# A two-layer Hyena and attention block whose instructions are put in order by the scheduler's timeline model

## The chip, the cores and the metric

The kernel runs on one core of a Trainium2 chip. The core has five engines that each work through a queue of their own in order: PE (TensorE, matrix products), DVE (VectorE), ACT (ScalarE), POOL (GpSimd) and SP (SyncE, which here only issues DMAs). They meet through semaphores. The metric is the device time of one execution in microseconds (us); a kernel's time is the median of its runs.

## What is computed

The reference is a block of two layers over 512 latent tokens and 256 context tokens of width 1024, in float32. Layer 0 is a Hyena mixer (a long convolution by FFT), layer 1 is grouped-query attention. Cut to its core:

```python
def hyena_mixer(h, w_in, conv_w, conv_b, ..., d_skip, w_out):
    proj = h @ w_in                                       # 1024 -> 4 x 2048
    x0, x1, v = split(short_conv(proj[..., :3 * E_HY], conv_w, conv_b), 3)
    z = proj[..., 3 * E_HY:]
    u = x1 * v
    k = hyena_filter(L, ...)                              # per channel, over |k| summed
    y = irfft(rfft(u, 2 * L) * rfft(k, 2 * L))[:L]
    y = (y + u * d_skip) * x0
    return (y * silu(z)) @ w_out

def gqa_mixer(h_lat, h_ctx, w_in, q_g, k_g, w_out):
    q, k, v, z = ...                                      # 16 heads of 128, 4 key heads
    q, k = rope(rms_norm(q)), rope(rms_norm(k))           # context keys carry no position
    o = softmax(q @ k_all.T / sqrt(128)) @ v_all          # 512 queries, 768 keys
    return (o * silu(z)) @ w_out

def reference(x, c, ctx, c_ctx, ...):
    for i in range(2):
        sh, sc, gt = split(silu(c) @ ada_w[i] + ada_b[i], 3)
        h = rms_norm(x, norm_g[i]) * (1 + sc) + sh        # the same for ctx with c_ctx
        x = x + gt * (hyena_mixer if i == 0 else gqa_mixer)(h, ...)
    return x
```

## The kernel before

A float32 matrix is carried as two fp32r parts, a high and a low one, and a product is three matmuls: high by high, high by low, low by high. In the input projection of the Hyena layer (`in_step`, L465 to L470) one step of the contraction is therefore six matmuls, three of 512 columns for the latents (tile `pl...`) and three of 256 for the context (`pc...`), and eight steps make one projection of 128 channels. ACT makes the high part of a weight (`whi`, L121), POOL the low part (`wlo`, L122).

**The Hyena layer** runs over eight groups g of 256 channels, each of two chunks i = 2g, 2g+1 of 128. A group is one period of some 99 us, from about 100 to 850 us of the profile. In a period PE computes for each chunk the projections `plx1`, `plv`, `plz`, `plx0`. The short convolution behind each (`conv`) is one ACT instruction (L512) and four DVE instructions (L513 and L515, each for latents and context), which read the projection out of its bank of PSUM. u = x1 v is transposed (`ut`, L537 and after) and brought to the frequency domain (`pu`, `fwd`, L550). The filter of the next group is made beside it: `pk` (`lags`, L377 to L382, six per group), a norm (`knorm`, L395, a DVE reduction), folding on POOL (F, L428 to L435) and its transform `ks` (L441, ending in DVE's `kt`, L452). DVE multiplies spectra (`ab...`, `times`, L560, then L584) and folds them (`Y`, L569, L570); `pq` (`y_stage`, L616) is the way back, ACT scales its second half (`qs`, L624), DVE adds and subtracts (L625, L626) and finishes y (L628, L629). The modulation vectors of the second layer are summed on DVE in this stretch too (`adaacc`, L198), from 512-KB pieces that SP fetches (`adas`).

**Two rings of four PSUM banks** feed these: `mmt` (L157) for the projections, `axt` (L160) for everything else, `pk`, `ks`, `ut`, `pu` and `pq` among it. A tile that takes a bank waits until the readers of the tile that had it four tiles earlier are through:

```python
    def axt(name):
        return pa.tile([P, 512], F32, tag="ax", name=name, bufs=4)
```

**The attention layer** (about 1000 us to the end) runs over eight pairs p of heads, 64 blocks n of 128 queries. `score` (L1088) computes `sc` on PE, DVE takes the row maximum (L1099, L1100), ACT the exponential `E` with its sum (L1102), DVE divides (L1103, L1104). `turn` (L1107) transposes E on PE (`et`, L1114), ACT copies it to `pth` (L1118) and DVE takes the low part `ptl` (L1119). `mix` (L1121) multiplies two such blocks with the values (`po`). Projections for later pairs (`pq`, `pz`) and the output product (`px`) stand between. `sc` and `et` share a ring of two PSUM tiles (`s3`, L995), so a score waits for the tile used two before it, and E has two buffers.

**The order.** The program is written as one stream in which the stages of a period are laid by hand between the steps of the projections (a table of slots at the loop over g). That stream is not the order on the engines: the framework's `TileContext` collects all instructions, its scheduler chooses an order for each engine's queue, and only then are buffers' waits turned into semaphores. In the kernel before, the scheduler goes by a plain list of ready times. The engines then follow the order chosen, strictly, each its own queue.

## Time and profile before

| | us |
|---|---|
| runs | 1512.92, 1518.78, 1520.66 |
| median | 1518.78 |
| the profiled execution, its own time | 1517.56 |
| its span, first to last instruction | 1515.7 |
| PE busy | 1455.5 (96%) |
| DVE busy | 1183.7 (78%) |
| ACT busy | 547.5 (36%) |
| POOL busy | 513.9 (34%) |
| mean granted TensorE clock, share of full | 0.983 |

Busy is the time in which an engine had an instruction under way. Matmuls are pipelined: of two back to back of 512 columns the second starts 0.23 us after the first, though each is shown with 0.39 to 0.40 us, so PE's idle time is shorter than the distance between two starts. TensorE's clock has two levels, 2.4 and 1.2 GHz, written as 1.00 and 0.50; a number between them is a mean over a stretch. "Idle before" is the time in which an engine had nothing under way, and the releaser is the instruction that ended it.

### The profile page before, as it was taken

What the parts mean: (1) busy time and instruction counts of PE and PEld (TensorE: products, weight loads), DVE (VectorE), ACT (ScalarE), POOL (GpSimd) and SP (SyncE); (2) the same over time, 40 slices, a digit from 0 to 9 for tenths busy, and PEclk for the clock granted to TensorE, in tenths of its full rate; (3) what the DMA queues carried; (4) which work ended last, traced back from release to release, by engine and by line L of the source; (5) the groups of instructions that cost most, each with busy time, mean ns of one, the idle gap of its engine ahead of it and who ended that gap; (6) DMA issues with size and microseconds to landing.
All of it is one profiled execution on the core that took longest, in us unless ns stands there. A gap on an engine that the chain in (4) does not pass through costs nothing.

```text
span 1515.7 us, 22866 instructions
## 1 busy us (share of the span) xinstructions
PE 1455.5 (96%) x8787; PEld 1263.9 (83%) x8787; DVE 1183.7 (78%) x2004; ACT 547.5 (36%) x1057; POOL 513.9 (34%) x449
## 2 busy tenths in 40 slices
PE   8998999989999999999999999999999999999998
PEld 1787987878878878789888787799998998998987
DVE  5769879889789888987969644575787878878886
ACT  3431322313223223223232334543545544544542
POOL 2462744626537354264464343121110000000005
PEclk9999999999999999999999999999999999999999
DMA  8612223232232232223233667246232212212111
GB/s 298 189 50 83 78 77 91 77 93 86 74 105 69 85 87 70 87 85 90 84 98 108 236 218 260 72 123 214 85 112 70 82 58 70 84 57 70 44 64 74
DMA packets 150783, 157.45 MB, mean 104 GB/s; under 512 B 6953, under 2 KB 122212, under 8 KB 150164
## 3 DMA queue, kind: packets, MB, share of 16 engines
q1 hardware_dynamic: 146324, 134.76, 28.7%
q0 software_dynamic: 4208, 20.72, 4.0%
q8 instruction: 69, 1.13, 0.3%
q10 hardware_dynamic: 144, 0.52, 0.1%
q14 instruction: 38, 0.31, 0.1%
HBM read 138.14 MB, written 17.84 MB: 103 GB/s over the span
## 4 chain that ended last, share of the span: by engine, by line
PE 60%; DVE 23%; issue 5%; POOL 5%; DMA 4%; ACT 2%; SPq 0%; POOLq 0%; ACTq 0%; DVEq 0%
PE po L70 4%; PE po L72 4%; PE po L71 4%; DVE adaacc L198 3%; PE et L1114 3%; DMA adas<-in_ada_w_dram 2%; PE px L70 2%; PE pz L70 2%; PE px L72 2%; PE pz L72 2%; PE px L71 2%; PE pz L71 2%; PE pq L70 2%; PE pq L72 2%; PE pq L71 2%
## 5 line engine op out<-in xcount | busy, mean ns | idle before, releaser
L122 POOL TENSOR_TENSOR wlo<-stg,whi 128x1024 fp32r<-128x1024 f32 x64 | 159.3, 2489 | 260.9 <-ACT whi L121 256.6
L121 ACT CAST whi<-stg 128x1024 fp32r<-128x1024 f32 x99 | 103.8, 1049 | 233.6 <-PE pcz L468 81.1
L873 POOL TENSOR_TENSOR r2q<-s2q,mhalf 128x2 f32<-128x2 f32 x32 | 23.4, 731 | 343.6 <-DVE s2q L871 332.4
L465 PE MATMUL plx<-h_hi,whi 128*128 128x512 f32 x248 | 104.1, 420 | 8.1 <-DVE cvx L515 8.1
L198 DVE SCALAR_TENSOR_TENSOR adaacc<-adas,sil,adaacc 128x512 f32<-128x512 f32 x98 | 102.8, 1053 | 10.9 <-DMA adas<-in_ada_w_dram 10.6
L1102 ACT ACTIVATE E<-sc,st 128x768 f32<-128x768 f32 x64 | 57.7, 902 | 126.9 <-DVE st L1100 114.1
L469 PE MATMUL plx<-h_hi,wlo 128*128 128x512 f32 x248 | 101.3, 409 | 0.0
L466 PE MATMUL plx<-h_lo,whi 128*128 128x512 f32 x248 | 101.3, 408 | 0.0
L467 PE MATMUL pcx<-hc_hi,whi 128*128 128x256 f32 x248 | 72.5, 292 | 4.7 <-DVE cvx L515 4.6
L1099 DVE TENSOR_REDUCE st<-sc 128x1 f32<-128x768 f32 x64 | 61.0, 953 | 17.5 <-PE sc L72 17.2
L468 PE MATMUL pcx<-hc_lo,whi 128*128 128x256 f32 x248 | 71.7, 289 | 0.0
L470 PE MATMUL pcx<-hc_hi,wlo 128*128 128x256 f32 x248 | 71.5, 288 | 0.0
L752 DVE TENSOR_TENSOR yl<-yf,yh 128x768 fp32r<-128x768 f32 x26 | 25.7, 990 | 51.9 <-ACT yh L751 51.8
L1119 DVE TENSOR_TENSOR ptl<-et,pth 128x768 fp32r<-128x768 f32 x64 | 61.1, 954 | 5.3 <-ACT pth L1118 4.0
L465 PEld LDWEIGHTS plx<-h_hi,whi 128*128 128x128 f32 x248 | 49.2, 198 | 18.7 <-issue 8.8
L467 PEld LDWEIGHTS pcx<-hc_hi,whi 128*128 128x128 f32 x248 | 49.2, 198 | 18.5 <-issue 4.9
L1118 ACT CAST pth<-et 128x768 fp32r<-128x768 f32 x64 | 51.1, 798 | 31.1 <-PE et L1114 31.0
L468 PEld LDWEIGHTS pcx<-hc_lo,whi 128*128 128x128 f32 x248 | 49.1, 198 | 11.3
L465 PE MATMUL plv<-h_hi,whi 128*128 128x512 f32 x120 | 49.4, 412 | 5.5 <-DVE cvv L515 5.5
L72 PE MATMUL po<-pth,kvt 128*128 128x256 f32 x192 | 54.1, 282 | 0.0
L71 PE MATMUL po<-ptl,kvt 128*128 128x256 f32 x192 | 54.0, 281 | 0.0
L70 PE MATMUL po<-pth,kvt 128*128 128x256 f32 x192 | 53.9, 281 | 0.0
(909 smaller groups left out, 5181.5 us busy)
## 6 DMA issues: line engine op xcount, KB each, us to landing
stg<-in_hy_w_in_dram SPq DMA_DIRECT2D x64, 512.0 KB
stg<-in_at_w_in_dram SPq DMA_DIRECT2D x40, 512.0 KB
adas<-in_ada_w_dram SPq DMA_DIRECT2D x32, 512.0 KB
yf<-y_scr POOLq DMA_DIRECT2D x32, 384.0 KB, 5.0
ad<-in_ada_w_dram SPq DMA_DIRECT2D x16, 512.0 KB
stg<-in_hy_w_out_dram SPq DMA_DIRECT2D x16, 512.0 KB
stg<-in_at_w_out_dram SPq DMA_DIRECT2D x16, 512.0 KB
dec<-in_k_dec_dram SPq DMA_DIRECT2D x48, 128.0 KB
```

Source lines behind the costliest of these rows:

```text
L70: TE.matmul(ps, lh, rh, start=first, stop=False)
L71: TE.matmul(ps, lh, rl, start=False, stop=False)
L72: TE.matmul(ps, ll, rh, start=False, stop=last)
L121: S.copy(hi, st)
L122: (lo_eng or lo_default[0]).tensor_tensor(lo, st, f(hi), ALU.subtract)
L198: V.scalar_tensor_tensor(accs[n_], sv[:, k, :], sc, accs[n_], ALU.mult, ALU.add)
L465: TE.matmul(pl, hi[:, k, :], h_hi[:, k, :], start=fi, stop=False)
L466: TE.matmul(pl, hi[:, k, :], h_lo[:, k, :], start=False, stop=False)
L467: TE.matmul(pc[:, 0:LC], hi[:, k, :], hc_hi[:, k, :], start=fi, stop=False)
L468: TE.matmul(pc[:, 0:LC], hi[:, k, :], hc_lo[:, k, :], start=False, stop=False)
L469: TE.matmul(pl, lo[:, k, :], h_hi[:, k, :], start=False, stop=la)
L470: TE.matmul(pc[:, 0:LC], lo[:, k, :], hc_hi[:, k, :], start=False, stop=la)
```

## The change

The context in which the program is recorded gets one flag. With it the scheduler orders each block against its timeline model, a model of when each engine would start and end each instruction, in place of the plain list of ready times.

```diff
-    with tile.TileContext(nc) as tc:
+    with tile.TileContext(nc, schedule_with_timeline_sim=True) as tc:
         hybrid_kernel(tc, *args, out)
```

No instruction is added, removed or reshaped: both programs have 8473 on PE, 2006 on DVE, 884 on ACT, 454 on POOL and 384 on SP. What differs is the place of each in its queue, and with it the semaphores. Three places follow. Names of tiles end in a running number; the part ahead of it is the name in the code with its group, chunk or block.

**PE, at the `pk` of group 4** (`plx0_7` is the projection of x0 for chunk 7, `plx1_8` that of x1 for chunk 8). Before:

```order
L469 MATMUL plx0_7_3955<-h_hi_69,wlo32_3951 128x512
L470 MATMUL pcx0_7_3956<-hc_hi_71,wlo32_3951 128x256
L379 MATMUL pk4_0_3998<-w4h4_3984,h3_194 128x512
L380 MATMUL pk4_0_3998<-w4l4_3985,h3_194 128x512
L379 MATMUL pk4_1_4004<-w4h4_3984,h3_194 128x512
L380 MATMUL pk4_1_4004<-w4l4_3985,h3_194 128x512
L465 MATMUL plx0_7_3955<-h_hi_69,whi32_3950 128x512
L466 MATMUL plx0_7_3955<-h_lo_70,whi32_3950 128x512
```

After, at the first and at the second `pk`:

```order
L465 MATMUL plx0_7_3955<-h_hi_69,whi32_3950 128x512
L466 MATMUL plx0_7_3955<-h_lo_70,whi32_3950 128x512
L379 MATMUL pk4_0_3998<-w4h4_3984,h3_194 128x512
L380 MATMUL pk4_0_3998<-w4l4_3985,h3_194 128x512
L467 MATMUL pcx0_7_3956<-hc_hi_71,whi32_3950 128x256
L468 MATMUL pcx0_7_3956<-hc_lo_72,whi32_3950 128x256
L469 MATMUL plx0_7_3955<-h_hi_69,wlo32_3951 128x512
```

```order
L470 MATMUL pcx1_8_4079<-hc_hi_71,wlo33_4074 128x256
L465 MATMUL plx1_8_4078<-h_hi_69,whi33_4073 128x512
L379 MATMUL pk4_1_4004<-w4h4_3984,h3_194 128x512
L380 MATMUL pk4_1_4004<-w4l4_3985,h3_194 128x512
L466 MATMUL plx1_8_4078<-h_lo_70,whi33_4073 128x512
L467 MATMUL pcx1_8_4079<-hc_hi_71,whi33_4073 128x256
L468 MATMUL pcx1_8_4079<-hc_lo_72,whi33_4073 128x256
```

Before, the second `pk` stands right behind the first. After, it stands 29 rows behind it, among the steps of the next projection; the remaining four follow at distances of 7 to 19 rows, where before it was 8.

**DVE, in the y step of chunk 6** (it reads `pq6` and finishes y; `mx4_0` is the norm's reduction of group 4, `cvx1_8` the short convolution that frees the bank of `plx1_8`). Before:

```order
L515 SCALAR_TENSOR_TENSOR cvx0_7_4064<-pcx0_7_3956,vb_81,cvx0_7_4064 128x255
L626 SCALAR_TENSOR_TENSOR y6_4126<-pq6_0_4112,rn_87,qs6_0_4127 128x2x128
L605 TENSOR_TENSOR cvx0_7_4064<-cvx0_7_4064,sz7_3946 128x768
L625 SCALAR_TENSOR_TENSOR y6_4126<-pq6_1_4113,rn_87,qs6_1_4131 128x128
L626 SCALAR_TENSOR_TENSOR y6_4126<-pq6_1_4113,rn_87,qs6_1_4131 128x128
L198 SCALAR_TENSOR_TENSOR adaacc_1_512_0_3697<-adas_1_512_3_4383,sil_82,adaacc_1_512_0_3697 128x512
L628 SCALAR_TENSOR_TENSOR y6_4126<-cvx1_6_3266,vb_81,y6_4126 128x768
L198 SCALAR_TENSOR_TENSOR adaacc_1_512_0_3697<-adas_1_512_3_4383,sil_82,adaacc_1_512_0_3697 128x512
L629 TENSOR_TENSOR y6_4126<-y6_4126,cvx0_6_3840 128x768
L198 SCALAR_TENSOR_TENSOR adaacc_1_512_1_3700<-adas_1_512_3_4383,sil_82,adaacc_1_512_1_3700 128x512
L395 TENSOR_REDUCE mx4_0_4428<-kfl4_3988 128x256
L513 SCALAR_TENSOR_TENSOR cvx1_8_4168<-plx1_8_4078,vb_81,cvx1_8_4168 128x511
```

After:

```order
L395 TENSOR_REDUCE mx4_0_4428<-kfl4_3988 128x256
L513 SCALAR_TENSOR_TENSOR cvx1_8_4168<-plx1_8_4078,vb_81,cvx1_8_4168 128x511
L513 SCALAR_TENSOR_TENSOR cvx1_8_4168<-pcx1_8_4079,vb_81,cvx1_8_4168 128x255
L382 TENSOR_TENSOR kfc4_3989<-pk4_5_4054,dec4_5_4052 128x512
L386 MEMSET kfc4_3989 1x256
L625 SCALAR_TENSOR_TENSOR y6_4126<-pq6_0_4112,rn_87,qs6_0_4127 128x2x128
L626 SCALAR_TENSOR_TENSOR y6_4126<-pq6_0_4112,rn_87,qs6_0_4127 128x2x128
L515 SCALAR_TENSOR_TENSOR cvx1_8_4168<-plx1_8_4078,vb_81,cvx1_8_4168 128x511
L515 SCALAR_TENSOR_TENSOR cvx1_8_4168<-pcx1_8_4079,vb_81,cvx1_8_4168 128x255
```

Before, the whole y step stands ahead of the convolution of `plx1_8`. After, the convolution's first half stands ahead of the y step and its second half behind the first two instructions of it; the `adaacc` rows have gone to an earlier place.

**PE, in the last pair of heads** (`sc63` is the last score, `et61` the transposes of block 61, `px6` the output product of pair 6). Before:

```order
L72 MATMUL px6_2_0_14741<-whx134_14472,ohl6_14076 128x512
L1114 MATMUL et61_14751<-ident_60,E61_14669 128x128 x6
L70 MATMUL px6_2_1_14774<-whi133_14466,ohl6_14076 128x512
L71 MATMUL px6_2_1_14774<-wlo133_14467,ohl6_14076 128x512
L72 MATMUL px6_2_1_14774<-whi133_14466,ohl6_14076 128x512
L70 MATMUL px6_2_1_14774<-whx134_14472,ohl6_14076 128x512
L71 MATMUL px6_2_1_14774<-wlx134_14473,ohl6_14076 128x512
L72 MATMUL px6_2_1_14774<-whx134_14472,ohl6_14076 128x512
L70 MATMUL po30_14784<-pth60_14706,kvt3_13089 128x256
L70 MATMUL px6_3_0_14818<-whi133_14466,ohl6_14076 128x512
L71 MATMUL px6_3_0_14818<-wlo133_14467,ohl6_14076 128x512
L70 MATMUL sc63_14760<-kvt3_13089,qh7_14063 128x512
```

After, from the last matmul of `sc62`:

```order
L71 MATMUL sc62_14727<-kvt3_13089,qh7_14063 128x256
L72 MATMUL sc62_14727<-kvt3_13089,ql7_14064 128x256
L1114 MATMUL et61_14751<-ident_60,E61_14669 128x128 x6
L70 MATMUL sc63_14760<-kvt3_13089,qh7_14063 128x512
L71 MATMUL sc63_14760<-kvt3_13089,qh7_14063 128x512
```

Before, products `px6` and the head of `po30` stand between `et61` and `sc63`, and six more `px6` between `sc62` and `et61`. After, `sc63` follows `sc62` with only `et61` between.

At the head, SP issues all loads of x and three further pieces (two of `dec`, and `kinv`) ahead of most pieces of `ad`, the first layer's modulation weights; before, these stood behind them. At the end, the last output products `px7` are finished close together instead of one after the other.

## Rows read from the trace of the kernel before

**Rows 1.** The page: span, busy time by engine, GB/s in 40 slices.

```profile
span 1515.7 us, 22866 instructions
...
PE 1455.5 (96%) x8787; PEld 1263.9 (83%) x8787; DVE 1183.7 (78%) x2004; ACT 547.5 (36%) x1057; POOL 513.9 (34%) x449
...
GB/s 298 189 50 83 78 77 91 77 93 86 74 105 69 85 87 70 87 85 90 84 98 108 236 218 260 72 123 214 85 112 70 82 58 70 84 57 70 44 64 74
```

**Rows 2.** Windows: stretch, length, busy us by engine, TensorE clock, DMA share, GB/s.

```profile
0.00:100.00 100.00, 89.64 (x386) 53.95 (x387) 67.12 (x122) 39.90 (x78) 46.72 (x60) 0.95 0.62 198
100.00:850.00 750.00, 707.15 (x4263) 621.83 (x4263) 641.99 (x856) 211.49 (x346) 360.98 (x258) 0.97 0.29 87
850.00:1000.00 150.00, 147.14 (x720) 121.38 (x720) 80.70 (x139) 65.06 (x112) 49.07 (x69) 1.00 0.55 186
1000.00:1516.00 516.00, 511.55 (x3424) 466.71 (x3422) 393.88 (x890) 231.03 (x521) 57.11 (x63) 1.00 0.27 86
```

**Rows 3.** Waits of PE: line, what released it; total us, times, longest.

```profile
PE plx L465 <- DVE cvx L515: 8.1, 4, 2.7
PE plv L465 <- DVE cvv L515: 5.5, 5, 3.4
PE pcx L467 <- DVE cvx L515: 4.6, 2, 3.4
PE pk L379 <- DVE ab411a L560: 3.2, 1, 3.2
...
PE pk L379 <- DVE ab211a L560: 1.7, 1, 1.7
```

**Rows 4.** Timeline of PE: start, duration, instruction, [idle before it <- releaser].

```profile
431.00 0.39 PE L465 MATMUL plx<-h_hi,whi 128*128 128x512 f32 x1
432.05 0.40 PE L465 MATMUL plx<-h_hi,whi 128*128 128x512 f32 x1
...
433.34 0.40 PE L380 MATMUL pk<-w4l,h 128*128 128x512 f32 x1
436.60 0.48 PE L379 MATMUL pk<-w4h,h 128*128 128x512 f32 x1 [2.87 <-DVE ab311a L560]
...
468.22 0.28 PE L470 MATMUL pcv<-hc_hi,wlo 128*128 128x256 f32 x1
471.16 0.77 PE L465 MATMUL plx<-h_hi,whi 128*128 128x512 f32 x1 [2.65 <-DVE cvx L515]
```

**Rows 5.** Windows on two stretches at a lower TensorE clock.

```profile
147.00:151.00 4.00, 4.00 (x15) 3.28 (x14) 4.00 (x7) 0.00 (x0) 0.00 (x0) 0.59 0.30 91
822.00:830.00 8.00, 6.55 (x22) 5.67 (x23) 7.96 (x9) 0.87 (x2) 3.92 (x2) 0.57 0.40 131
```

**Rows 6.** Timeline of DVE around the y steps of one period.

```profile
454.12 0.48 DVE L625 SCALAR_TENSOR_TENSOR y<-pq,rn,qs 128x256 f32<-128x256 f32 x1 [4.01 <-ACT qs L624]
...
457.82 3.51 DVE L628 SCALAR_TENSOR_TENSOR y<-cvx,vb,y 128x768 f32<-128x768 f32 x1
...
465.49 3.82 DVE L395 TENSOR_REDUCE mx<-kfl 128x256 f32<-128x2048 f32 x1
469.22 0.74 DVE L513 SCALAR_TENSOR_TENSOR cvx<-plx,vb,cvx 128x511 f32<-128x511 f32 x1
...
477.07 1.02 DVE L628 SCALAR_TENSOR_TENSOR y<-cvx,vb,y 128x768 f32<-128x768 f32 x1
```

**Rows 7.** Timeline of POOL in the same stretch.

```profile
458.12 2.39 POOL L122 TENSOR_TENSOR wlo<-stg,whi 128x1024 fp32r<-128x1024 f32 x1
```

**Rows 8.** Groups of DVE, 100 to 850 us: busy, mean ns, idle before.

```profile
L198 DVE SCALAR_TENSOR_TENSOR adaacc<-adas,sil,adaacc 128x512 f32<-128x512 f32 x96 | 100.8, 1054 | 10.9 <-DMA adas<-in_ada_w_dram 10.6
```

**Rows 9.** Timeline of DVE in attention.

```profile
1441.13 0.68 DVE L1064 TENSOR_TENSOR x<-x,px 128x512 f32<-128x512 f32 x1
...
1456.68 0.96 DVE L1099 TENSOR_REDUCE st<-sc 128x1 f32<-128x768 f32 x1 [0.19 <-PE sc L72]
...
1458.95 0.17 DVE L1103 RECIPROCAL st<-st 128x1 f32<-128x1 f32 x1 [1.12 <-ACT E L1102]
```

## The prediction

> **What bounds the kernel now.** I read the page first: PE is busy for 1455.5 of 1515.7 us [rows 1], so an order can give back at most PE's idle time and its time at the lower clock. The windows tell where these lie [rows 2]. From 100 to 850 us, the Hyena periods, PE is busy 707.15 of 750 us and idle 42.9; in attention it is idle 4.5 of 516, most of it behind the last matmul. So the stretch that can gain is Hyena, and attention can only lose. The list of PE's waits names the idle time [rows 3]: seven waits of `pk` for an `ab` product of DVE, from 3.2 to 1.7 us, sum 19.7; and waits of the projections for the convolution that frees their bank, 8.1 + 5.5 + 4.6 = 18.2. The rest, 5 us, is scattered. The timeline then shows one of each kind [rows 4]: PE stands from 433.34 to 436.60 at the second `pk`, and from 468.22 to 471.16 at a `plx`.
>
> Neither is a lack of DVE time: DVE is busy 642 of 750 us [rows 2], 84.8 in a period of 99.1 (7.57 of these in the stretch). It is the order of its queue. In the second case DVE idles 4.01 us for the `qs` of a y step, then works that step off, with one instruction of 3.51, and a reduction of 3.82, and only at 469.22 begins the convolution that PE needs [rows 6].
>
> The waits cost a second time. After each of the long waits (the shortest is 2.8 us) the granted clock falls to the lower of its two levels, 1.2 GHz, for a stretch. The first such stretch reads 0.59 over 4 us, or 1.6 us of full-speed work lost; the last, a double one, 0.57 over 6.55 us of work, or 2.8 [rows 5]. There are eleven from 100 to 850: 10 x 1.6 + 2.8 = 19 us. Waits of 1.8 us or less had none.
>
> **The change part by part.** Nothing is added or removed, so every term is a wait that goes, comes or grows. I set the sum against the profiled execution's 1517.6 us, 1.2 below the median of the runs. For a wait in the new order I add the durations that the trace gives to the instructions between the two points on both queues, and take what the waiting engine is early by.
>
> *Waits that go.* Before, the second `pk` stood right behind the first. Now 29 rows stand between, nearly five steps of six matmuls at 1.05 us each (431.00 to 432.05) [rows 4]: 5 us of PE work where 3.3 were stood idle. The convolutions now stand ahead of the y step or within it, so `plx` no longer waits behind the 4.0 of idle time, the 3.51 and what lies between [rows 6]. By this addition the Hyena waits left in the new order are five: 1.3 (a `pk`), 1.7 (a `pu`), 1.2 (a `ks`), 2.7 (the `po` at the end) and 1.7 (a `pq`), together 8.6.
>
> *Waits that come in Hyena.* The y step is later, and its two banks of the `axt` ring with it; that is in the 8.6. The sums of `adaacc` stand up to 35 rows earlier in DVE's queue, ahead of the `ab400a` products. They waited 10.6 us in all for their DMA before, over 96 instructions [rows 8]. Earlier in the queue they meet two pieces in series and DVE idles about 4.5 us a period there, an estimate from the issue of a piece to its first use, some 4 us. What reaches PE lies between nothing (DVE has 14 us of slack in a period) and 3.5 us a period, 24.5 in seven; I take 1 a period, 7 us, nearer the low end because the old waits of this kind, though 10.6 us long, name no wait of PE. The folding on POOL feeds `ks` with 0 to 1 us to spare; bounds 0 and 14 us, taken 2. Hyena idle time is then 8.6 + 7 + 2 = 17.6 in place of 42.9: **25 us less**.
>
> *The clock.* Waits long enough for a drop remain at the `po` and perhaps at two others: 4 us in place of 19, **15 less**. Bounds: 5 if a wait near 3 us stays in every period, 19 if none does.
>
> *Attention.* Here the new order is tighter. A score may begin when the exponential of the score before it has left their bank. From the end of `sc` to the end of E the trace shows about 2.4 us: the reduction begins 0.19 after PE at 1456.68, E is over at 1458.95 [rows 9]. Before, the PE work between one score and the next was 3.6 us or more in all but two places (2.3 and 1.6). Now it is 2.05 in seven places and 0.66 in three, where only the transposes stand between (and 1.4 where it was 1.6): 7 x 0.35 + 3 x 1.75 = 7.7. Three transposes (`et`) come 1.1 early and one `po` 1.0, together 4.3. **12 more.** Bounds: 6, if part of these waits gives DVE time that the next one uses, and 20, if the queue of DVE, busy 394 of 516 us [rows 2], runs late at some of the others. None is long enough for the clock.
>
> *Head, border and tail.* At the head some 0.5 MB more go ahead of the last `ad`: at the 298 GB/s of the first slice [rows 1] 1.7 us, bounds -1 and 2. From 850 to 1000 PE is idle 2.9 us [rows 2] and its order changes throughout: 0, bounds -2.9 and 3. At the end the last products finish together, with additions of 0.68 [rows 9] behind each other: 1, bounds 0 and 2. **3 more.**
>
> Sum: 1517.6 - 25 - 15 + 12 + 3 = 1492.6; with the 1.2 to the median, about 1494.
>
> *A rule against it.* DVE's L628 took 3.51 us at 457.82 and 1.02 at 477.07; beside the first, POOL was in a subtraction from 458.12 to 460.51 [rows 6, 7]. The Trainium skill (SBUF — State Buffer, "SBUF: two separate sides") says that a DVE instruction with two SBUF inputs and a GpSimd instruction that reads SBUF share a port pair which one holds for its whole length while the other waits. By that rule, the trace agrees: L628 ended at 461.33, 0.8 after POOL's instruction. An order that puts more of DVE's two-input work beside POOL then makes DVE slower, which the second rival prices.
>
> **The rivals.** *Best case:* only the 8.6 stay in Hyena, all dips go, attention loses 6, the edges nothing: 1517.6 - 34.3 - 19 + 6 = 1470, or 1471. For it: DVE's slack. Against: the waits for POOL and DMA.
>
> *DVE held up by POOL.* A period has six instructions like L628 (L605, L628, L629 of two chunks). If two more of them meet POOL, each adds 2.5 us [rows 6]: DVE at 89.8 a period, and with some 6 us of waits for ACT that the new order doesn't take out, 96 of the 99.1. Hyena then gives 7.57 x 3.1 = 23 in place of 40, and the time is 1517.6 - 23 + 15 = 1510, or 1511. Against: the order of POOL changes little.
>
> *Attention becomes the loss* (slower). Place: the waits of `sc`, `et` and `po`. In the new order 39 of 263 stand under 1 us of slack; before it was 14. If DVE comes to each of the 39 a time x later than this addition says, the kernel loses 39x more. It is slower by over 0.5% from 25 + 7.6 = 39x on, x = 0.84 us; at x = 1.2 the time is 1492.6 + 47 = 1540. For it: DVE's busy share. Against: one `L1099` is 0.96 us [rows 9], and DVE would need such a piece ahead at nearly every place.
>
> *It doesn't do what it says:* the model's durations differ from the chip's so much that new waits of the old size appear elsewhere in Hyena: 1515 to 1522.
>
> **How the numbers follow.** The forecast 0.50, the best case 0.18, POOL 0.17, attention 0.10, no effect 0.05. A measurement of this kernel can tell about 0.5% from no change, 7.6 us: under 1511.2 is faster, over 1526.4 slower. Faster: 0.48 of the first, 0.18, and half of the third, 0.08: 0.74. Slower: attention 0.10, and 0.03 of the others. Same: 0.13. The range reaches from just under the best case to the POOL case with the edges' bounds added: 1468 to 1518, with some 0.05 below and 0.13 above. The predicted time is the forecast's, 1494.
>
> **What would show it right or wrong.** Right: PE idle for 15 to 22 us in 100 to 850 in place of 42.9 (the stretch will end some 35 us earlier), no `pk` wait over 2 us, the `cv` waits gone, two to four stretches at the lower clock; in attention some ten waits of 0.4 to 1.8 us at `sc` and `et` in the last pair of heads. Wrong: waits of `ks` for POOL or of `pu` for `utl` of 2 us in every period; L605, L628 and L629 with means over 2.5 us; idle time of PE in attention over 30 us.

## The result and the profile after

The changed kernel takes 1537.8 us (median of 4 runs, 1536.1 to 1541.9); the kernel before took 1517.6 beside it. The ratio is 1.0139, with an interval of 1.0113 to 1.0165: **slower by 1.4%**, where 1494 was forecast with a range of 1468 to 1518.

First the page of the changed kernel, then its windows (stretch, length, busy us by engine, TensorE clock, DMA share, GB/s), the counterparts of [rows 1, 2].

```profile
span 1536.9 us, 22874 instructions
...
PE 1465.3 (95%) x8787; PEld 1264.9 (82%) x8787; DVE 1169.1 (76%) x2004; ACT 546.9 (36%) x1057; POOL 504.0 (33%) x449
```

```profile
0.00:100.00 100.00, 89.32 (x357) 51.58 (x358) 64.12 (x120) 38.68 (x76) 40.06 (x55) 0.91 0.59 193
100.00:850.00 750.00, 716.63 (x4338) 626.67 (x4337) 636.30 (x864) 216.19 (x355) 363.56 (x266) 0.99 0.30 89
850.00:1000.00 150.00, 142.99 (x714) 120.18 (x713) 76.55 (x136) 63.15 (x115) 45.87 (x68) 0.98 0.54 184
1000.00:1516.00 516.00, 499.52 (x3288) 452.01 (x3288) 381.34 (x869) 226.62 (x509) 49.31 (x58) 0.99 0.25 81
```

PE's idle time fell from 42.9 to 33.4 us in Hyena. It rose from 2.9 to 7.0 at the border, and from 4.5 to 16.5 in the window from 1000 us on, behind which another 21 us of the span now lie. The list of PE's waits (line, releaser; total us, times, longest), beside [rows 3], says at what:

```profile
PE pq L616 <- DVE Y L569: 7.0, 4, 3.3
PE po L70 <- ACT yh L751: 6.8, 1, 6.8
PE et L1114 <- DVE st L1100: 6.3, 3, 2.3
PE po L70 <- DVE ab711a L560: 5.9, 1, 5.9
PE sc L70 <- ACT E L1102: 4.3, 7, 0.7
...
PE pq L616 <- DVE y L626: 2.7, 5, 0.8
PE po L71 <- DVE st L1100: 2.0, 1, 2.0
PE po L70 <- ACT pth L1118: 2.0, 6, 0.4
```

Of the 18.2 us of `cv` waits of [rows 3] 1.6 us are left, and the longest `pk` wait is now 1.1. None of the lines above was in that list: each is new. Two single waits are of about 6 and 7 us, one at the end of Hyena (`ab711a`) and one at the border (`yh`).

This table, read from the timelines of PE, gives how far each kernel is behind the kernel before at the start of the same matmul (us; negative is ahead). The middle columns are two of the experiments below.

| PE begins (at a y step: its last matmul) | changed | its order alone | new Hyena alone |
|---|---|---|---|
| first projection (L465; before at 52.2) | +5.2 | +7.0 | +0.3 |
| y step of chunk 4 (350.3) | +11.4 | +7.7 | +4.4 |
| y step of chunk 12 (747.6) | -10.3 | -19.3 | -21.8 |
| last projection (L470, 834.1) | -17.0 | -26.2 | -28.6 |
| last y step (L616, 850.8) | -7.7 | -17.9 | -16.7 |
| first transposes of attention (1062.2) | -1.5 | -12.3 | -16.1 |
| transposes of block 48 (1409.5) | +8.0 | -2.9 | -16.1 |
| last matmul (1511.5) | +21.0 | +9.8 | -16.1 |

So the changed kernel loses 5.2 at the head, gains 22.2 over the projections, and gives 15.5 back between the last projection and attention. It loses 9.5 in the 48 blocks and 13.0 in the last two pairs of heads. The new Hyena alone gains nothing up to chunk 4 (it goes from +0.3 to +4.4), then 26.2 over the four periods to chunk 12, 6.5 each, and gives 5.1 back by the last y step. The last projection overstates a lead: with the old order under the flag (below) it came 8.8 early in the profile and the last y step 1.3.

### The profile page after: what moved, and what is told of

Same layout as the page of the kernel before. It is cut to its first block, busy times and chain, and to the rows that moved or that the text cites. A ratio compares the mean times of both kernels' runs of the same rounds, so it can differ in the third digit from the quotient of the medians.

```text
span 1536.9 us, 22874 instructions
## 1 busy us (share of the span) xinstructions
PE 1465.3 (95%) x8787; PEld 1264.9 (82%) x8787; DVE 1169.1 (76%) x2004; ACT 546.9 (36%) x1057; POOL 504.0 (33%) x449
## 5 line engine op out<-in xcount | busy, mean ns | idle before, releaser
L122 POOL TENSOR_TENSOR wlo<-stg,whi 128x1024 fp32r<-128x1024 f32 x64 | 165.2, 2582 | 233.8 <-ACT whi L121 233.8
L198 DVE SCALAR_TENSOR_TENSOR adaacc<-adas,sil,adaacc 128x512 f32<-128x512 f32 x98 | 96.5, 1017 | 45.9 <-DMA adas<-in_ada_w_dram 45.7
L465 PE MATMUL plx<-h_hi,whi 128*128 128x512 f32 x248 | 99.1, 400 | 1.0 <-DVE cvx L515 1.0
L1102 ACT ACTIVATE E<-sc,st 128x768 f32<-128x768 f32 x64 | 57.7, 902 | 65.5 <-DVE st L1100 64.9
L1099 DVE TENSOR_REDUCE st<-sc 128x1 f32<-128x768 f32 x64 | 60.9, 952 | 14.5 <-PE sc L72 14.5
L470 PE MATMUL pcx<-hc_hi,wlo 128*128 128x256 f32 x248 | 69.5, 280 | 0.0
L616 PE MATMUL pq<-kinv,Y 128*128 128x128 f32 x384 | 51.5, 284 | 12.1 <-DVE Y L569 7.0
L616 PEld LDWEIGHTS pq<-kinv,Y 128*128 128x128 f32 x384 | 47.2, 194 | 16.0 <-DVE Y L569 7.7
L1118 ACT CAST pth<-et 128x768 fp32r<-128x768 f32 x64 | 51.1, 799 | 26.3 <-PE et L1114 26.2
L1114 PE MATMUL et<-ident,E 128*128 128x128 f32 x384 | 52.9, 275 | 6.3 <-DVE st L1100 6.3
L122 DVE TENSOR_TENSOR wlo<-stg,whi 128x1024 fp32r<-128x1024 f32 x35 | 42.8, 1222 | 20.2 <-ACT whi L121 14.2
L70 PE MATMUL po<-pth,kvt 128*128 128x256 f32 x192 | 55.7, 290 | 2.0 <-ACT pth L1118 2.0
L465 PEld LDWEIGHTS plx<-h_hi,whi 128*128 128x128 f32 x248 | 47.0, 190 | 10.9 <-ACT ko0m L449 1.1
```

The costliest lines, as they stand in the source:

```text
L70: TE.matmul(ps, lh, rh, start=first, stop=False)
L122: (lo_eng or lo_default[0]).tensor_tensor(lo, st, f(hi), ALU.subtract)
L198: V.scalar_tensor_tensor(accs[n_], sv[:, k, :], sc, accs[n_], ALU.mult, ALU.add)
L465: TE.matmul(pl, hi[:, k, :], h_hi[:, k, :], start=fi, stop=False)
L616: TE.matmul(dst, ysp[g, b, jt][:, cs * 256 + j * P:cs * 256 + (j + 1) * P], kinv[:, jt, cs, :], start=jt == 0, stop=jt == 1)
L1114: TE.transpose(tp_[:, b * P:(b + 1) * P], E[:, b * P:(b + 1) * P], ident)
```

## The experiments

All tables below lay the queues of the five engines out by hand: each instruction gets an order-only edge to the one that the table puts ahead of it, as in this edit. A table can hold the changed kernel's order, the old one, or one up to a point of PE's queue (with what that needs on the other queues) and the other from there.

```diff
-    with tile.TileContext(nc, schedule_with_timeline_sim=True) as tc:
+    with tile.TileContext(nc) as tc:
         hybrid_kernel(tc, *args, out)
+        _pin(tc, nc)   # for each queue: add_manual_dep(instruction, the one ahead, NoSync)
```

### Which part of the order gains, which loses

**The order alone.** The table holds the changed kernel's order, without the flag.

> The flag is off; the order that the timeline model chose is laid on each engine's queue by a table instead, every instruction tied behind the one ahead of it. If the order is all that the flag changes, this runs as the changed kernel, 1536 to 1542 us, with PE waiting for the same instructions. If the flag did something else too (other waits, other buffers), the time lies nearer to that of before, 1518.

Measured: 1527.4 us, ratio 1.008 (1.0052 to 1.0109), 10.4 less than the changed kernel. The flag thus does more than order: in the built program nine pairs of neighbouring pieces that are loaded have also changed places among the three `stg` buffers, and a few tiles of other rings have changed theirs. The wait of `pq` for `Y`, 7.0 in the changed kernel, is shorter here:

```profile
PE pq L616 <- DVE Y L569: 1.9, 3, 1.0
```

**New order until Hyena's last projection, old from there:**

```diff
-_ORDER = the changed kernel's
+_ORDER = the changed kernel's up to the last L470, then the old
```

> The new order up to the last matmul of the Hyena projections and what that needs, the old order from there to the end. First theory: each stage's time goes with its own order. By the two traces the head costs 5.2 more, Hyena from the first to the last projection 22.2 less, so 1517.6 + 5.2 - 22.2 = 1501 us; up to 1509 where work that the new order had put before that point is done after it. Rival: the Hyena gain is only work taken early, which is paid behind it: 1517 or more.

Measured: 1503.1, ratio 0.991 (0.9885 to 0.9934).

**Old order until the first transposes of attention, new from there:**

```diff
-_ORDER = the changed kernel's
+_ORDER = the old up to the first L1114, then the changed kernel's
```

> The old order up to the first transposes of attention (et of block 0), the new one from there. First theory: attention's loss lies in its own order, 22.5 us by the two traces from that point to the end: 1517.6 + 22.5 = 1540 us. Rival: attention is late because of what the new order leaves behind at the border (weights and buffers that come later): then 1518 to 1525 here.

Measured: 1544.5, ratio 1.0185 (1.016 to 1.0211). In its profile 2.5 us are lost ahead of the first transposes and 23.8 from there to the last matmul, so attention's new order alone costs about 24 us; the same waits of `et`, `sc` and `po` stand in its list.

**New order for Hyena alone:**

```diff
-_ORDER = the changed kernel's
+_ORDER = the old up to the first L465, the changed kernel's up to the last L470, then the old
```

> The old order up to the first projection, the new one through Hyena, the old one again from its last projection on. First theory: the head's 5.2 us go away beside e2: 1496 us, up to 1504. Rival: as in e2, 1512 or more; a second rival, that the late start of the head was made good in Hyena by slack anyway, gives the same time as e2.

Measured: 1500.6, ratio 0.989 (0.9859 to 0.9919). Hyena gains 16 us (1517.0 less 1500.6). Of the head's 5 to 7 us only 2.5 (1503.1 less 1500.6, and 2.4 in the profiles) reach the end; the intervals of the two ratios overlap.

**The flag with the old order, and with the new Hyena alone.** The flag stays on, and the table holds the old order in the first, the order of the last run in the second:

```diff
     with tile.TileContext(nc, schedule_with_timeline_sim=True) as tc:
         hybrid_kernel(tc, *args, out)
+        _pin(tc, nc)
```

> The flag is on, and the old order is laid on each queue by the table. The pinned new order without the flag ran at 1527 us and not at 1538, so the flag does something besides the order; the rows of the two programs differ in which of the three buffers of the ring stg a piece of weights takes. First theory: that costs only where the new order leaves the queues no slack, so the old order runs as before, 1514 to 1520 us. Rival: the buffers chosen under the flag cost some 10 us in any order: 1525 to 1530.

Measured: 1516.0, ratio 0.9997 (0.9981 to 1.0013).

> The spliced order of e4, laid on with the flag on, so that the scheduler chooses the buffers as in the changed kernel. First theory: the adas pieces then take the buffer that DVE frees in place of the one that POOL frees, come later, and Hyena loses what the pinned order lost, 8 to 10 us: 1508 to 1511. Rival: those 10 us came from elsewhere (head, border, chance): 1500.

Measured: 1506.4, ratio 0.9925 (0.9904 to 0.9946). At one and the same order the flag costs 5.8 us in the new Hyena (four runs each, 1498.1 to 1501.5 without it and 1504.7 to 1509.8 with it) and nothing in the old. The buffers are the only difference found between the two programs; that they are what costs is not shown, since no run changed the buffers alone.

### Attention

In the last pair `sc` follows the score before it with only `et` between. DVE and PE there, in the changed kernel (start, duration, instruction, [idle before it <- releaser]):

```profile
1493.94 0.96 DVE L1099 TENSOR_REDUCE st<-sc 128x1 f32<-128x768 f32 x1
1494.82 0.95 DVE L1119 TENSOR_TENSOR ptl<-et,pth 128x768 fp32r<-128x768 f32 x1
```

```profile
1493.63 0.28 PE L72 MATMUL sc<-kvt,ql 128*128 128x256 f32 x1
1495.91 1.00 PE L1114 MATMUL et<-ident,E 128*128 128x128 f32 x6 [2.01 <-DVE st L1100]
```

The releaser is named by the last semaphore. What `et` needs is `ptl` of the block before, which reads the bank that `et` overwrites; it stands on DVE behind the row maximum (L1099) of the score that has only just begun, so PE waits for both instructions, 0.96 and 0.95 us. The three `et` and one `po` of this pair make 8.3 us. Behind three of these four waits stands a stretch at the lower clock (behind all four in the run with the old order until attention), as in this window:

```profile
1496.00:1500.00 4.00, 3.95 (x15) 3.15 (x16) 2.45 (x4) 1.71 (x3) 0.46 (x1) 0.57 0.00 0
```

**The old order for the last two pairs:**

```diff
-_ORDER = the changed kernel's
+_ORDER = the changed kernel's up to block 48's transposes, then the old
```

> The new order, without the flag, up to the transposes of block 48, the old order for the rest (the last two pairs of heads). By the traces this stretch takes 114.8 us in the pinned new order and 102.0 in the old. First theory: the loss is made there and goes: 1527.4 - 12.8 = 1515 us. Rival: the old order finds its inputs late behind the new one and loses as much: 1525 or more.

Measured: 1512.6, ratio 0.9973 (0.9959 to 0.9987): 14.8 us less than the order alone.

**`ptl` ahead of the row maximum** at the three places, on DVE:

```diff
+L1119 TENSOR_TENSOR ptl_14508<-et_14509,pth_14507 128x6x128
 L1099 TENSOR_REDUCE st_14531<-sc_14524 128x1
-L1119 TENSOR_TENSOR ptl_14508<-et_14509,pth_14507 128x6x128
```

> The pinned new order with one exchange at three places of the last pair: on DVE the low part ptl of block n goes ahead of the row maximum of score n+2, in place of behind it. First theory: the transposes of block n+1 wait for the buffer that ptl reads, behind a row maximum of 0.95 us: three waits of 2.2 us become 1.2, and one or two stretches at the lower clock go, 3 to 7 us in all: 1520 to 1524. Rival: the transposes wait for their own exponential (as the row names st): no gain or a loss, since the row maximum of the next score is later, 1527 to 1530.

Measured: 1527.2, no gain. In place of three waits of 2.0 to 2.4 at `et` there are these, of `et` for `ptl` itself, shorter by one DVE instruction, and of the next score for the exponential, later by the same instruction:

```profile
PE sc L70 <- ACT E L1102: 4.5, 4, 1.3
PE et L1114 <- DVE ptl L1119: 2.9, 3, 1.0
```

Removing one DVE instruction from ahead of one wait put it ahead of the next. Score, row maximum, exponential, transposes and `ptl` form one chain from bank to bank; the PE work between the blocks, which the old order had, hid it, and with the old order for these pairs the waits and the loss are gone (the run before this).

**The score six matmuls earlier on PE**, once a pair, for the waits of `sc`:

```diff
+L70 MATMUL sc_11139<-kvt_9701,qh_10523 128x512
 ... the five others of this score
 L70 MATMUL px_3_0_11206<-whi_10712,ohl_10104 128x512
 ... the five others of this product
-L70 MATMUL sc_11139<-kvt_9701,qh_10523 128x512
```

> The pinned new order with the last score but one of each of six pairs of heads put six matmuls earlier on PE, ahead of one block of the output product (1.4 us of work), so that the score behind it stands 3.4 in place of 2.05 us of PE work after it. First theory: the wait of the score for the exponential before it, 0.84 a pair, goes, the wait of 0.48 behind it stays: 1527.4 - 5 = 1522 us. Rival: the wait moves to the score that was put earlier, or to po, and nothing is gained: 1527.

Measured: 1527.0, no gain. The rows of DVE and ACT show why. The score ends on PE before 1262.6, but the row maximum stands on DVE behind an addition that waits for a product, and the exponential on ACT behind a cast:

```profile
1262.26 0.28 PE L72 MATMUL sc<-kvt,ql 128*128 128x256 f32 x1
```

```profile
1263.96 0.69 DVE L1064 TENSOR_TENSOR x<-x,px 128x512 f32<-128x512 f32 x1 [1.76 <-PE px L72]
1264.57 0.95 DVE L1099 TENSOR_REDUCE st<-sc 128x1 f32<-128x768 f32 x1
```

```profile
1264.66 1.06 ACT L121 CAST whi<-stg 128x1024 fp32r<-128x1024 f32 x1 [5.63 <-PE px L72]
1265.74 0.90 ACT L1102 ACTIVATE E<-sc,st 128x768 f32<-128x768 f32 x1
```

**The whole chain earlier**: the row maximum ahead of that addition on DVE (in five of the six pairs), the exponential ahead of the cast on ACT as well.

```diff
-L1064 TENSOR_TENSOR x_3_10695<-x_3_10695,px_3_0_11835 128x512
 L1099 TENSOR_REDUCE st_11773<-sc_11766 128x1
 L1100 TENSOR_SCALAR st_11773<-st_11773 128x1
+L1064 TENSOR_TENSOR x_3_10695<-x_3_10695,px_3_0_11835 128x512
```

> As e8, and the score's whole chain is put earlier: on DVE the row maximum of that score goes ahead of the addition of an output product (L1064) that stood in front of it, on ACT its exponential goes ahead of a cast of weights (L121, 1.05 us). Putting the score alone earlier moved nothing: its row maximum waited in DVE's queue for that addition, its exponential behind that cast. First theory, in place of the one that fell: the order of DVE and ACT, not of PE, makes the wait of the next score; now it goes, 0.84 to 0.97 a pair, six pairs: 1527 - 5 = 1522 us, a pair takes 57.5 us in place of 58.6. Rival: the weights cast later, or the addition, are late for their reader: 1527 or more.

Measured: 1525.7, ratio 1.0056. From block 0 to 48 the kernel is 3.7 us faster than the order alone (57.7 us a pair in place of 58.6; the old order takes 56.7). Up to 1460 us 0.4 us of the 4.1 us of `sc` waits is left, so these waits were this one chain; they are 3.7 of the 9.4 us that the 48 blocks lose. The time as a whole fell by 1.8, and the intervals of the two ratios overlap.

### Hyena: do PE's waits pace it?

The prediction priced the waits of PE. These three take them out of the *old* order by hand: the second to sixth `pk` later on PE; the convolution of `plx` ahead of L628 on DVE; both.

```diff
 L380 MATMUL pk_0_1294<-w4l_1281,h_194 128x512
+ ... three steps of six matmuls (plx_1, pcx_1), which stood behind pk_2
 L379 MATMUL pk_1_1300<-w4h_1280,h_194 128x512
```

> The old order, and only the second to sixth pk of each period are moved on PE, behind three steps of the projection and then one step apart; nothing is moved on another engine. First theory: PE sets the pace, the 3 us that it stood idle are filled, seven waits (19.7 us) and the stretches at the lower clock behind them (some 10 us) go: 1516 - 20 to 30 = 1486 to 1496 us. Rival: DVE sets the pace, and what PE gains it waits for a few us later (plx, plv or pq): 1508 to 1516.

Measured: 1520.8, ratio 1.0033 (1.0018 to 1.0049).

```diff
-L628 SCALAR_TENSOR_TENSOR y_1422<-cvx_0_647,vb,y_1422 128x768
-L395 TENSOR_REDUCE mx_0_1724<-kfl_1284 128x256
-L629 TENSOR_TENSOR y_1422<-y_1422,cvx_0_1136 128x768
 L513 ... and L515 of cvx_2_1464<-plx_2_1374, pcx_2_1375
+L628, L395 and L629 as above
```

> The old order, and only on DVE the four instructions of the convolution of x1 (L513, L515) go ahead of L628 of the y step, 4 to 8 rows earlier, in seven periods. First theory: the waits of plx and pcx for them (12.7 us, and of plv, 5.5, in part) and the lower clock behind them go: 1516 - 13 to 25 = 1491 to 1503 us. Rival: y is later by 2.3 us, and the banks or the products behind it are waited for in its place: 1512 or more.

Measured: 1514.3, ratio 0.9987 (0.9971 to 1.0003). The third has both edits:

> Both moves, of e10 and e11, in the old order. If PE sets the pace, the gains add up, 33 to 55 us: 1461 to 1483. If the new order's gain in Hyena (16 us to the end, 22 to the last projection) is all that DVE leaves, this stops at the same place, 1495 to 1503 us, and PE waits at the end of Hyena for the products of DVE as in e4.

Measured: 1515.8, ratio 0.9992 (0.9976 to 1.0008); neither of the two expected times came. The largest waits of the first and of the third, and PE's window from 100 to 850 of each of the three:

```profile
PE plx L465 <- DVE cvx L515: 21.2, 7, 4.9
```

```profile
PE plv L465 <- DVE cvv L515: 20.7, 6, 4.1
```

```profile
100.00:850.00 750.00, 708.05 (x4247) 621.01 (x4247) 661.81 (x855) 209.62 (x345) 363.41 (x258) 0.97 0.29 87
```

```profile
100.00:850.00 750.00, 709.61 (x4284) 624.56 (x4284) 632.45 (x861) 214.30 (x351) 364.69 (x259) 0.97 0.29 88
```

```profile
100.00:850.00 750.00, 709.47 (x4273) 622.84 (x4272) 651.24 (x859) 211.60 (x349) 364.99 (x257) 0.97 0.29 87
```

A wait of `pk` that was filled came back as one of `plx`; with `plx` mended too, as one of `plv`. PE is busy for 708 to 710 of 750 us each time, as before (707.15, [rows 2]). Every wait over 1.0 us in this window is for DVE: in the old order the loop through DVE's queue sets the period, and PE's idle time is what that leaves.

In the new order DVE does the same instructions in less time. Three of its groups before, and these with L198 in the changed kernel, from 100 to 850 (busy us, mean ns | idle before; L198 before is in [rows 8]):

```profile
L605 DVE TENSOR_TENSOR cvx<-cvx,sz 128x768 f32<-128x768 f32 x16 | 31.7, 1981 | 0.0
L629 DVE TENSOR_TENSOR y<-y,cvx 128x768 f32<-128x768 f32 x15 | 29.7, 1979 | 0.3
L628 DVE SCALAR_TENSOR_TENSOR y<-cvx,vb,y 128x768 f32<-128x768 f32 x15 | 27.0, 1799 | 0.3
```

```profile
L198 DVE SCALAR_TENSOR_TENSOR adaacc<-adas,sil,adaacc 128x512 f32<-128x512 f32 x96 | 95.0, 1023 | 45.9 <-DMA adas<-in_ada_w_dram 45.7
L629 DVE TENSOR_TENSOR y<-y,cvx 128x768 f32<-128x768 f32 x16 | 26.3, 1641 | 0.5
L605 DVE TENSOR_TENSOR cvx<-cvx,sz 128x768 f32<-128x768 f32 x16 | 24.8, 1548 | 0.0
L628 DVE SCALAR_TENSOR_TENSOR y<-cvx,vb,y 128x768 f32<-128x768 f32 x16 | 23.6, 1474 | 0.4
```

Over all DVE instructions of Hyena the sum of durations fell from 722 to 710 us (708 in the new Hyena alone). More idle time for `adas` (45.7 in place of 10.6) took the place of DVE's waits for ACT's `uth` and `qs`, which are 4.4 and 3.5 us in the changed kernel and before were:

```profile
DVE utl L543 <- ACT uth L542: 45.4, 14, 5.1
...
DVE y L625 <- ACT qs L624: 23.0, 17, 4.0
```

From the first products (L560) of group 1 to those of group 7, six periods, DVE takes 586.5 us before and 565.4 in the new Hyena alone: 16.4 less work and 4.7 less idle. That the shorter work is the cause is not shown, and two runs speak against it. With the convolution moved in the old order (the second of the three above) the same stretch has 11.1 less work, but 5.4 more idle time, and takes 580.7; the time gained 1.7 us. With all sums late (below) the work is the least, 483.4 in place of 488.0, and that kernel is 5.7 us slower than the new Hyena alone. How much of Hyena's gain comes from shorter instructions, and how much from the work that now stands where DVE waited for `uth` and `qs`, is open.

**The sums of `adaacc` later.** In the new Hyena alone, those between `utl` and the second product go behind it; in the next run also those ahead of `utl`.

```diff
 L543 TENSOR_TENSOR utl_1600<-ut_4_1931,uth_1599 128x2x128
-L198 ... six sums from adas, two by two between the rows below
 L560 TENSOR_TENSOR ab100a<-pu_0_0_1959,kt_1750 128x1024
 L560 TENSOR_TENSOR ab100b<-pu_1_0_1972,kt1m_1513 128x1024
 L584 TENSOR_TENSOR ab100a<-ab100a,ab100b 128x1024
 ...
 L560 TENSOR_TENSOR ab101a<-pu_0_0_1959,kt1p_1643 128x1024
+L198 ... the six sums
```

> As e4 (old head, new Hyena, old rest, 1500.6 us), and on DVE the sums adaacc (L198) that stand between the last utl and the second ab product group of each period go behind the product ab01a, two to six rows later; they wait for the second adas piece, 2.9 and 3.5 us of DVE idle time in two periods looked at. First theory: DVE's queue sets Hyena's pace and these waits are on it: up to 3 us a period, 10 to 20 us in all, 1481 to 1491 us. Rival: the products wait for PE's pu there anyway, or the piece's buffer comes free later and the next weights with it: 1497 to 1504.

Measured: 1499.6, ratio 0.9876 (0.9854 to 0.9898), the same as without the move.

> As e13, and the two to four sums ahead of utl, which wait 1.8 us for the first adas piece, go behind the same product. First theory: 1.8 us a period more, 1475 to 1488 us. Rival: DVE then waits for uth (ACT) at utl as it did in the old order (37 us in six periods), and the time is that of e13 or worse.

Measured: 1506.3, ratio 0.992 (0.9903 to 0.9937), slower. The group L198 in the first and the second:

```profile
L198 DVE SCALAR_TENSOR_TENSOR adaacc<-adas,sil,adaacc 128x512 f32<-128x512 f32 x96 | 93.0, 1008 | 21.1 <-DMA adas<-in_ada_w_dram 20.9
```

```profile
L198 DVE SCALAR_TENSOR_TENSOR adaacc<-adas,sil,adaacc 128x512 f32<-128x512 f32 x96 | 78.7, 862 | 2.0 <-DMA adas<-in_ada_w_dram 1.7
```

In the second DVE no longer idles for `adas`, and PE waits at two other places, which the new Hyena alone has for 1.0 us and not at all:

```profile
PE plx L465 <- DVE cvx L515: 6.5, 5, 1.7
...
PE pu L70 <- DVE ab501b L560: 2.8, 1, 2.8
```

So DVE's idle time at `adas`, four times that of before, was not what held Hyena: at the early place the sums wait while DVE would have waited for PE or ACT anyway. In the second DVE's idle time over the six periods is 83.1 us in place of 77.5, and from 150 to 740 us waits for `uth` of 18.3 in place of 1.7 are back.

### Where Hyena's lead goes at its end

In the new Hyena alone the lead is 28.6 at the last projection and 16.7 at the last y step, 29 us later. PE stands twice there:

```profile
811.95 0.77 PE L70 MATMUL po<-whi,yhl 128*128 128x512 f32 x1 [5.26 <-DVE ab711a L560]
821.29 0.77 PE L70 MATMUL po<-whi,yhl 128*128 128x512 f32 x1 [3.25 <-DVE cvx L515]
```

**The old order for the last Hyena period, or the last two**, behind the new ones:

```diff
-_ORDER = old, the changed kernel's up to the last L470, old
+_ORDER = old, the changed kernel's up to the y steps of chunk 13 (or of chunk 11), old
```

> The old order at the head, the new one until the end of the y steps of chunk 13, the old one from there (the last Hyena period, border, attention); buffers as before. In the new Hyena order with the old rest (1500.6) PE stood 5.3 us for the last `ab711a` and 3.3 us for a `cv` behind it, and each was followed by a stretch of some 6.8 us at the lower clock. Theory: these waits belong to the way the new order ends Hyena (the last `ab` products far back in DVE's queue). With the old ending they go, some 8.6 us and 4 to 6 for the clock, and the old period's own waits of about 5 us come back: 1490 to 1496. Rival: they are DVE's backlog, which has to be paid wherever the projections end, and the old ending shows waits of the same sum at other places: 1499 to 1504.

Measured: 1499.7, ratio 0.9862 (0.9829 to 0.9896).

> As the kernel with the old last period, but the old order begins behind the y steps of chunk 11, one period of about 99 us earlier. Theory: one more period at the old pace (99.2 in place of 93.7) on top of the old ending: 1496 to 1502. Rival (backlog): the period gains nothing that isn't paid back, so it costs nothing to give it up: 1499 to 1504, and the same as the other of this pair within 2 us.

Measured: 1496.9, ratio 0.9851 (0.9822 to 0.988): the lowest median of all, below the kernel before by 1.5% and below the changed one by 2.7%. The intervals of these two and of the new Hyena alone (1500.6) overlap, so what follows rests on the profiles.

From the y step of chunk 12 to the last, the new Hyena alone loses 5.1 of its lead, the first of these 1.0 and the second none (-25.4 at both). So the ending of the new order does cost, but 4 to 5 us, not the 9 to 14 that the theory took from the two waits: with the old last period a `po` waits 5.4 for a `cvx` and a `pu` 2.4 for `utl`. The profiled head of the second was also 4.3 us ahead of the first's at the first y step, with one low-clock stretch fewer, so their medians' difference is not the ending alone.

### The border

The wait of `po` for `yh` (6.8 us) has its cause on POOL, in the changed kernel:

```profile
854.04 0.55 POOL L750 DMA_DIRECT2D yf<-y_scr  x1 [0.30 <-POOL yl L752]
867.51 0.45 POOL L818 TENSOR_TENSOR tbk<-ropeq,tbk 128x128 f32<-128x128 f32 x1 [12.92 <-DMA tbk<-in_at_q_g_dram]
...
871.42 1.64 POOL L750 DMA_DIRECT2D yf<-y_scr  x3
```

Three read-backs of y stand behind attention's table work (L818, L822), which stood 12.9 us for its own DMA. PE got the first tile at 877. **The three ahead of the tables again**, in the order alone:

```diff
 L750 DMA yf_8_7953<-y_scr 128x768
+L750 DMA yf_9_7977<-y_scr 128x768
+L750 DMA yf_10_8007<-y_scr 128x768
+L750 DMA yf_11_8048<-y_scr 128x768
 L818 TENSOR_TENSOR tbk<-ropeq,tbk 128x128
 ...
-the three L750
```

> The changed kernel's order with the old buffers (1527.4), but on POOL three read-backs of y (L750 of yf_9 to yf_11) stand ahead of the table work of attention (L818, L822) again, as in the kernel before. In the changed kernel POOL stood 12.9 us for the table's DMA at L818, and the three read-backs came out only behind it, at 871.4; PE waited 6.8 us for `yh` of the first of them, with a stretch of 6.8 us at the lower clock behind. Theory: this place in POOL's queue is the whole border loss; the wait of `po` for `yh` goes, and with it 6.8 us and about 3 for the clock: 1517 to 1521. Rival: the read-backs wait for the casts of the tiles ahead of them anyway (10.1 us in all at L750 for `yl`), so that the `po` comes late as before: 1524 to 1529.

Measured: 1524.0, ratio 1.0036 (1.0017 to 1.0056), 3.4 less than the order alone and short of the 1517 to 1521 expected; the two intervals just overlap. The wait for `yh` is gone, and this is the largest that stands in its stretch:

```profile
PE po L70 <- DVE res L770: 2.1, 1, 2.1
```

From the last y step to the first transposes the kernel before takes 211.4 us, the order alone 217.0, this one 212.5. So the place of the read-backs in POOL's queue is 4.5 of the 5.6 us that are lost between these two points.

## Why the prediction was wrong

**What bounds the kernel.** That only Hyena could gain and attention only lose was right. The next sentence, "Neither is a lack of DVE time", failed: it took DVE's busy share for slack. DVE was idle in its queue, behind ACT, PE and DMA, and in the old order that loop is the period. Filling PE's waits alone moved the time by 0.3% at most (three runs).

**Waits that go** (25 us with the clock apart). The named waits did go. But the addition treated them as independent, each worth its length, and PE's idle time fell by 9.5 in the window of 750 us. The new order's steady periods are 93.7 us in place of 99.2 in the new Hyena alone, close to what the forecast implies (40 us over 7.57 periods, 5.3 each). But that holds from chunk 4 to chunk 12 only: up to chunk 4 nothing was gained, though two `pk` waits of 3.1 us had gone there too, and the end gave 5.1 back. So Hyena with its clock, forecast at 40, gave 16 when it alone had the new order. The end of Hyena was sized 2.7 for a `po` and measured 5.9.

**`adas`.** DVE's idle time was estimated at 4.5 us a period and measured 35 more over Hyena, 5 a period. The 7 us that were put on PE's path are 0: taking half of the idle time away brought nothing, taking all of it cost 6.

**The clock** (15 less). From 100 to 850 the time at the lower level (1.2 GHz) fell from 41.0 to 17.1 us, as forecast in kind. But it came back elsewhere: at the head 17.1 in place of 10.2, at the border 6.8 in place of none, in attention 10.2 in place of 0.1. Over the whole span it is 51 us in both, and the mean granted clock is 0.983 in both: nothing was gained, not 15. The step that failed is "None is long enough for the clock", and no term stood for the clock at the head and the border. The waits that it was read from were a little shorter than the prediction says: one of 2.65 [rows 4] had its stretch at 471, so "the shortest is 2.8" is not right. After the 6.8-us wait at the border:

```profile
870.00:875.00 5.00, 0.27 (x2) 0.00 (x0) 0.00 (x0) 0.00 (x0) 3.06 (x8) 1.00 0.55 152
875.00:882.00 7.00, 4.96 (x11) 3.64 (x12) 2.12 (x3) 2.85 (x4) 0.54 (x1) 0.52 0.97 344
```

**Attention** (12, bounds 6 and 20; measured 22.5, and 23.8 alone). The three `et` and the one `po` were the right places, and of the ten `sc` seven wait, six of them 0.7: 4.3 us in place of 7.7, since in the last pair the `et` ahead takes the wait. The `et` and the `po` were sized 1.1 and 1.0 and measured 2.1 and 2.0, since the addition went to the exponential and left out that DVE takes the next row maximum [rows 9] ahead of `ptl`. Six waits of `po` at `pth` (2.0) and one at `qtp` (1.5) were not forecast. All named waits together are 16.1 us; with three stretches at the lower clock, at the prediction's price of 1.6 each, that makes 21 of the 22.5.

**Head, border and tail** (3). The head is late by 5.2, not 1.7; some 2.5 of it lasts. The border was set to 0 "since its order changes throughout"; POOL's queue was not read there, and it holds 4.5.

**What was in no term.** The flag itself costs 6 to 10 us beyond the order, by the difference of two pairs of runs.

In sum, from the table: +5.2 - 22.2 + 15.5 + 9.5 + 13.0 = 21.0, against -25. The slower rival had the right place but not the right mechanism: DVE is not late by some x at each of 39 places, it is late by one instruction at four, and the seven waits of `sc` are 0.6 each in the mean. That its 1540 lies near the 1537.8 measured is luck: attention lost 22.5 us and not 59. Of the three signs of being wrong none showed, and of those of being right the idle time did not (33.4 in place of 15 to 22) and the `et` waits were over 1.8.

DVE held up by POOL went the other way: L605, L628 and L629 took 17 to 22% less. The Trainium skill (SBUF — State Buffer, "SBUF: two separate sides") says that a DVE instruction with two SBUF inputs and a GpSimd instruction that reads SBUF share a port pair that one holds while the other waits. The trace agrees in that these are such instructions and that each of the three groups is 0.3 to 0.4 us shorter in the mean in the new order. The timelines of DVE and POOL show it by the single instruction. An L198 with no POOL instruction under way beside it took 0.73 to 0.75 us in both kernels (46 of 98 before, 66 in the changed kernel), one beside a POOL instruction 1.33 and 1.58 in the mean and up to 3.4. An L515 of 511 columns, which reads PSUM, took 0.73 to 0.74 in the mean with POOL beside it and without. So in the new order fewer of these sums meet POOL (of the folds L569 more do, 17 of 48 in place of 4); no run took POOL's work away.

Open stays what makes Hyena's periods shorter, why the flag's buffers cost what they do, and why the head's loss of 5 to 7 us shrinks to 2.5.

## What to carry to other kernels

Where every wait of the busy engine is for one other engine, price the loop through that engine's queue, not the waits: in three runs here a wait that was filled reappeared at the next thing that this queue hands over. Less work on that engine is no gain by itself either: where it was shortened in the old order, most of it came back as idle time. Read a new order at the joints between stages and on the queues that only issue DMAs, and follow a bank to the last instruction that reads it, not to the one that the score needs. An order is best taken apart: here the new order from the first projection to chunk 11 was worth 1.5%, and the rest of it, with the flag, cost 2.7%.

## What the runs showed of the hardware that was not expected

The lower clock level came behind waits in every stage, but not behind each: in the changed kernel three waits of 2.0 to 2.3 us in attention each had a stretch of 3.4 us behind them, a fourth of 2.0 (at 1483.5) had none, though the same wait had one in the run with the old order until attention, and the 5.9-us wait of a `po` had one of 6.8. The DVE instruction L198 took 1054 ns in the mean at the old place, 1023 in the changed kernel and 862 with all sums late, the same instruction with the same shape. Alone it took 0.73 to 0.75 us in each of the three; what the order changes is how many run beside a POOL instruction: 52 of 98 over the whole span, 32 and 17.
